# The first MLP product by pairs of feature chunks in seven block products instead of eight, with the residual kept in DRAM

## The chip, the cores and the metric

The kernel runs on one core of one Trainium2 chip. The metric is the device time of one execution in microseconds (us), as the median of three runs. A core has TensorE (PE in the profile, its weight loads apart as PEld), VectorE (DVE), ScalarE (ACT), GpSimd (POOL) and SyncE (SP, which here only issues transfers). Each runs its own list of instructions in a fixed order, and waits where an operand is not there yet.

## The reference

Two trunk layers run over 640 tokens (512 latent, 128 context) with 1024 features. What matters here is the second half of each layer, the MLP, and the modulation vectors that come from a product with `ada_w`:

```python
def ada_params(cond, w, b):
    m = jax.nn.silu(cond) @ w + b              # w: 1024 x 6144 for each layer
    return jnp.split(m[..., None, :], 6, axis=-1)
def mlp(h, w1, b1, w2, b2):                    # w1: 1024 x 4096, w2: 4096 x 1024
    return jnp.square(jax.nn.relu(h @ w1 + b1)) @ w2 + b2
for layer in range(2):
    ...                                        # mixer (even layer) or neighbourhood attention (odd)
    hp = modulate(xp, mp[3], mp[4])            # layer norm, times 1 + scale, plus shift
    hs = modulate(xs, ms[3], ms[4])
    xp = layer_norm(ALPHA * xp + mp[5] * mlp(hp, w1[layer], ...), ...)
    xs = layer_norm(ALPHA * xs + ms[5] * mlp(hs, w1[layer], ...), ...)
```

## The kernel before

All numbers are float32. Each operand of a product is split into a rounded part ("hi", type fp32r) and what the rounding left ("lo"), and a product is made of three matmuls: hi weights by hi data, hi by lo, lo by hi.

**Weights.** They come from DRAM in units of 128x1024 float32 (512 KB) in the order of a list (`stream_plan`). SP loads a unit into one of 3 `raw` slots; ACT copies it, rounded, into one of 4 `sp` slots (L170), and DVE subtracts the copy from the unit to get the lo half (L171). Up to two split units stand ready (`AHEAD`).

**The MLP** (`mlp`, L1026) of a layer runs over four blocks b of 1024 hidden features. Eight chunks m of 128 features of the first product come first: for a chunk, `ws` does 8 slices of 128 input features by 3 matmuls by 2 groups of tokens (384 and 256 columns), 48 matmuls in all; ACT adds the bias (L1020), DVE makes the squared ReLU (L1022), ACT and DVE split the result (`split_to`, L294 and L297). Then come 8 units of the second product (`tok_k_outer`, 30 matmuls of 512 columns for a unit). Its results are multiplied by a gate on DVE out of PSUM (L490) and added on POOL into the residual `x`, which lies in an SBUF slot R (L493): `evac_gated`. In the last block a `tail` does the second product together with the layer norm.

**The start of an MLP.** In block 0 the parts of chunks 0 to 3 for the first 384 tokens are computed first, while the last transposes and splits of the input `hT` (two R slots) still run. Then the gates are loaded, `make_base` scales the residual and adds the gated bias (POOL L504 twice, DVE L506 five times), and the 256-column rests of chunks 0 to 3 and the whole chunks 4 to 7 follow.

**The modulation of layer 1.** While layer 0's MLP runs, `ada_sum_gen` works through 48 steps, one for each weight unit: a 128x1024 piece of `ada_w` is loaded into an `n` slot, and DVE multiplies it by a factor and adds it to a sum, for two conditions (L428 for the first piece of a sum, then L430). Two loads stand ahead of the step at work. The R, `n` (6) and `vec` (4) slots of SBUF and the 8 banks of PSUM are given out by hand, a released slot going to the next user.

## Time and profile before

| | |
|---|---|
| median of three runs | 1514.3 us (1513.08 to 1514.66) |
| profiled execution, its own time | 1518.29 us |
| its span in the trace | 1516.2 us |
| PE busy | 1464.1 us, 97% of the span |
| DVE, ACT, POOL busy | 850.8, 594.4, 286.1 us |
| granted TensorE clock, mean | 0.984 |

The span is the time from the first to the last instruction in the trace; 2.1 us of the execution lie around it. Busy time is a sum over the whole program; what a stretch is worth has to be read from that stretch.

### The profile page before, as it was taken

Reading aid. Unit: us, or ns where it says so; the run is one execution under the profiler, and the core shown is the slowest. Engines: PE = TensorE matmul, PEld = TensorE weight load, DVE = VectorE, ACT = ScalarE, POOL = GpSimd, SP = SyncE. Lnnn points to the kernel's source line nnn. Section 1 sums busy time; section 2 is a strip of 40 time slices with the busy share of each in tenths; the row PEclk is TensorE's granted clock in tenths of the full one; section 3 lists DMA queues with packets and bytes.
Section 4 is the critical chain, followed back from the end, with each engine's and each line's share of the span. In section 5 each row is a group of like instructions: output and inputs, shape, how many; then the busy total and the mean of one; then the engine's idle time right before and its main releaser. Section 6 shows DMA issues by size and latency. Waiting matters only on the chain.

```text
span 1516.2 us, 21740 instructions
## 1 busy us (share of the span) xinstructions
PE 1464.1 (97%) x8572; PEld 1266.9 (84%) x8572; DVE 850.8 (56%) x1541; ACT 594.4 (39%) x1061; POOL 286.1 (19%) x327
## 2 busy tenths in 40 slices
...
GB/s 384 148 164 172 306 108 146 152 194 106 196 151 112 196 147 89 84 97 30 209 106 105 60 136 60 161 109 42 127 82 77 77 78 76 74 79 84 70 56 70
DMA packets 56373, 186.60 MB, mean 123 GB/s; under 512 B 10440, under 2 KB 10824, under 8 KB 56272
## 3 DMA queue, kind: packets, MB, share of 16 engines
...
q0 software_dynamic: 832, 1.09, 0.2%
...
## 4 chain that ended last, share of the span: by engine, by line
PE 76%; DVE 11%; ACT 5%; issue 4%; POOL 2%; DMA 2%; SPq 0%; POOLq 0%; DVEq 0%; ACTq 0%
PE bank L210 74%; DVE sp L171 2%; PE bank L1212 1%; POOL ln L514 1%; ACT R L755 1%; DVE R L506 1%; DVE R L297 1%; DVE R L495 1%; ACT junk L512 1%; DVE R L526 1%; DVE ln L533 1%; DVE acc L430 1%; ACT n L567 1%; DVE n L524 1%; POOL n L1202 1%
## 5 line engine op out<-in xcount | busy, mean ns | idle before, releaser
L210 PE MATMUL bank<-R,sp 128*128 128x384 f32 (+1 forms) x4368 | 664.5, 311 | 10.7 <-POOL R L296 3.6
L210 PEld LDWEIGHTS bank<-R,sp 128*128 128x128 f32 x4368 | 642.7, 190 | 28.4 <-issue 7.5
L210 PE MATMUL bank<-sp,R 128*128 128x512 f32 x2580 | 613.4, 396 | 7.1 <-DVE sp L171 2.6
L210 PEld LDWEIGHTS bank<-sp,R 128*128 128x128 f32 x2580 | 484.2, 189 | 128.3 <-issue 8.2
L171 DVE TENSOR_TENSOR sp<-raw,sp 128x1024 fp32r<-128x1024 f32 (+1 forms) x177 | 219.1, 1240 | 171.5 <-ACT sp L170 166.8
L170 ACT ACTIVATE sp<-raw 128x1024 fp32r<-128x1024 f32 (+1 forms) x177 | 186.1, 1056 | 316.0 <-PE bank L210 299.0
L493 POOL TENSOR_TENSOR R<-R,n 128x512 f32<-128x512 f32 x60 | 91.0, 1551 | 499.8 <-DVE n L490 499.8
L1022 DVE SCALAR_TENSOR_TENSOR n<-n 128x640 f32<-128x640 f32 x64 | 52.6, 822 | 189.3 <-ACT n L1020 189.3
L1020 ACT ACTIVATE n<-bank,pack 128x384 f32<-128x384 f32 (+1 forms) x128 | 61.2, 524 | 234.0 <-PE bank L210 228.4
L430 DVE SCALAR_TENSOR_TENSOR acc<-n,cx,acc 128x1024 f32<-128x1024 f32 x84 | 110.5, 1352 | 7.4 <-DMA n<-in_ada_w_dram 7.4
L297 DVE TENSOR_TENSOR R<-n,R 128x640 fp32r<-128x640 f32 (+2 forms) x123 | 98.6, 805 | 14.1 <-POOL R L296 11.1
L490 DVE TENSOR_TENSOR n<-bank,vec 128x512 f32<-128x512 f32 x100 | 67.3, 685 | 40.7 <-PE bank L210 36.6
L294 ACT ACTIVATE R<-n 128x640 fp32r<-128x640 f32 (+1 forms) x88 | 61.6, 704 | 44.3 <-DVE n L1022 39.5
L514 POOL TENSOR_TENSOR ln<-ln,mhalf 128x1 f32<-128x1 f32 x35 | 20.1, 575 | 296.8 <-DVE ln L513 296.8
L512 ACT ACTIVATE junk<-R,ln 128x1024 bf16<-128x1024 f32 x35 | 40.3, 1151 | 84.7 <-DVE ln L522 60.2
L210 PE MATMUL bank<-R,R 128*128 128x512 f32 x240 | 62.5, 405 | 0.0
L1202 POOL TENSOR_SCALAR n<-n,mx 128x384 f32<-128x384 f32 (+1 forms) x80 | 43.1, 541 | 91.1 <-DVE mx L1199 46.8
L567 ACT ACTIVATE n<-bank,mod 128x128 f32<-128x128 f32 x120 | 45.3, 455 | 26.5 <-PE bank L560 26.5
L210 PEld LDWEIGHTS bank<-R,R 128*128 128x128 f32 x240 | 44.4, 188 | 11.0
L1216 ACT ACTIVATE n<-bank 128x384 f32<-128x384 f32 (+1 forms) x80 | 32.9, 448 | 49.8 <-PE bank L1212 43.4
L1187 DVE CUSTOM_DVE_ANT_0 n<-bank,vec 128x256 f32<-128x256 f32 (+3 forms) x128 | 40.4, 350 | 13.2 <-PE bank L210 8.9
L1192 ACT ACTIVATE n<-n,mx 128x384 f32<-128x384 f32 x64 | 38.8, 610 | 20.4 <-DVE mx L1190 16.9
...
## 6 DMA issues: line engine op xcount, KB each, us to landing
raw<-in_wts_dram SPq DMA_DIRECT2D x184, 512.0 KB, 3.2
n<-in_ada_w_dram SPq DMA_DIRECT2D x80, 512.0 KB, 4.4
vec<-in_rpb_dram SPq DMA_DIRECT2D x16, 512.0 KB, 3.9
R<-in_ada_dram SPq DMA_DIRECT2D x15, 512.0 KB, 10.0
vec<-in_vecs_dram SPq DMA_DIRECT2D x13, 512.0 KB, 5.3
vec<-gscr SPq DMA_DIRECT2D x10, 512.0 KB, 4.8
R<-in_x_dram SPq DMA_DIRECT2D x5, 512.0 KB, 5.0
R<-in_xg_dram SPq DMA_DIRECT2D x5, 512.0 KB, 5.9
```

Of the source, the lines that this page charges most:

```text
L170: self.nc.scalar.activation(s.t[:, 0, :cols], r.t[:, :cols], AF.Copy)
L171: self.nc.vector.tensor_tensor(out=s.t[:, 1, :cols], in0=r.t[:, :cols], in1=s.t[:, 0, :cols].bitcast(F32), op=OP.subtract)
L210: self.nc.tensor.matmul(out, lhsT, rhs, start=start, stop=stop)
L294: self.nc.scalar.activation(hi, src, AF.Copy)
L297: (self.nc.vector if lo_eng == "dve" else self.nc.gpsimd).tensor_tensor(out=lo, in0=src, in1=hi.bitcast(F32), op=OP.subtract)
L430: nc.vector.scalar_tensor_tensor(acc.t[:, cond, :], w.t, f, acc.t[:, cond, :], op0=OP.mult, op1=OP.add)
L490: nc.vector.tensor_tensor(out=tmp.t[:, :512], in0=o.t, in1=gates[t // 4].t[:, c], op=OP.mult)
L493: nc.gpsimd.tensor_tensor(out=x[:, t, c], in0=x[:, t, c], in1=tmp.t[:, :512], op=OP.add)
L512: nc.scalar.activation(self.junk, src, AF.Square, bias=m[:, 2:3], accum_out=m[:, 4:5])
L567: nc.scalar.activation(dst, tr.t[:, j * 128:(j + 1) * 128], AF.Identity, bias=sh, scale=sc)
L1020: nc.scalar.activation(v[:, c0:c1], o.t[:, :c1 - c0], AF.Identity, bias=b)
L1202: nc.gpsimd.tensor_scalar(p.t[:, :n], p.t[:, :n], m[:, 5:6], 1.0, op0=OP.mult, op1=OP.mult)
```

## The change

The chunks m of 6 and above of each layer's first product (26 a layer, so 13 pairs a layer and 26 in all) are computed by pairs. For a pair the product is taken as 2x2 blocks: two chunks of 128 features, two halves of the 1024 input features, two halves of the 640 tokens. Seven block products of Winograd's form replace eight (`w1_pair`). A block product is 4 slices by 3 matmuls of 320 columns, so a pair has 84 matmuls where two chunks had 96. Around that:

- `split_pair`: a pair's two units become three and a half: POOL forms four 128x512 sums and differences in `vec` slots, and these are split too (ACT L172, DVE L173). Three may stand ready.
- `token_sums`, once a layer, in block 0 before `make_base`: POOL adds the hi and lo of `hT` (8 times 128x640), DVE forms 8 differences, and these are split (ACT, DVE) into two further R slots.
- The block products are combined on DVE out of PSUM, seven instructions of 320 columns; one of a pair's two results is split with its subtraction on POOL.
- The R slots for that come from the residual: after `make_base` it goes to DRAM (`xsum`, ten transfers of 256 KB), each gated result of the second product is added to it there by an accumulating DMA that POOL issues (`evac_sum`), and it is loaded back for the last block.
- The steps of `ada_sum_gen` run only within the second products of blocks 0 to 2 of layer 0, two for each unit. Of a step, one condition stays on DVE (L476, L479); for the other, ACT scales the piece and POOL adds it to the sum (128x1024, L481).

```diff
-ADA_MLP = 1
+ADA_MLP = 2
+PLAIN = 6
...
+    def paired(key):
+        return key[0] == "w1" and key[2] >= PLAIN
...
-        while len(self.ready) < self.AHEAD and (self.sp.free or self.extra) and self.raws:
-            r = self.raws.pop(0)
-            cols = 384 if self.plan[self.split_pos] == ("dft", 2) else 1024
+        while self.raws:
+            key = self.plan[self.split_pos] if self.split_pos < len(self.plan) else None
+            pair = self.paired(key)
+            if len(self.ready) >= (3 if pair else self.AHEAD) or not (self.sp.free or self.extra):
+                break
+            if pair and self.sub == 0 and len(self.raws) < 2:
+                break
             s = self.sp.get([128, 2, 1024], F32R) if self.sp.free else self.extra.pop(0)
-            with self.tc.high_priority(SPLIT_PRI):
-                self.nc.scalar.activation(s.t[:, 0, :cols], r.t[:, :cols], AF.Copy)
-                self.nc.vector.tensor_tensor(out=s.t[:, 1, :cols], in0=r.t[:, :cols],
-                                             in1=s.t[:, 0, :cols].bitcast(F32), op=OP.subtract)
-            r.done()
+            if pair:
+                self.split_pair(s)
+            else:
+                r = self.raws.pop(0)
+                cols = 384 if key == ("dft", 2) else 1024
+                self.split_unit(s, r.t, cols)
+                r.done()
+                self.split_pos += 1
...
+    def split_pair(self, s):
+        nc = self.nc
+        r = self.raws
+        if self.sub == 0:
+            r0, r1 = r[0].t, r[1].t
+            self.sums = [self.vec.get([128, 1024]) for _ in range(2)]
+            s1, s2 = (self.sums[0].t[:, i * 512:(i + 1) * 512] for i in range(2))
+            s3, s4 = (self.sums[1].t[:, i * 512:(i + 1) * 512] for i in range(2))
+            self.split_unit(s, r0, 1024)
+            nc.gpsimd.tensor_tensor(out=s1, in0=r1[:, :512], in1=r1[:, 512:], op=OP.add)
+            nc.gpsimd.tensor_tensor(out=s2, in0=s1, in1=r0[:, :512], op=OP.subtract)
+            nc.gpsimd.tensor_tensor(out=s3, in0=r0[:, :512], in1=r1[:, :512], op=OP.subtract)
+            nc.gpsimd.tensor_tensor(out=s4, in0=r0[:, 512:], in1=s2, op=OP.subtract)
+            r.pop(0).done()
+        elif self.sub < 3:
+            self.split_unit(s, self.sums[self.sub - 1].t, 1024)
+            self.sums[self.sub - 1].done()
+        else:
+            self.split_unit(s, r[0].t[:, 512:], 512)
+            r.pop(0).done()
+            self.split_pos += 2
+        self.sub = (self.sub + 1) % 4
...
-        if self.ada_every and self.seen % self.ada_every == 0:
+        for _ in range(self.ada_every):
             next(self.ada, None)
...
+            f = [self.s[:, k, cond:cond + 1] for cond in range(2)]
+            if k == 0:
+                nc.vector.tensor_scalar(acc.t[:, 0, :], w.t, f[0], None, op0=OP.mult)
+                nc.scalar.activation(acc.t[:, 1, :], w.t, AF.Copy, scale=f[1])
+            else:
+                nc.vector.scalar_tensor_tensor(acc.t[:, 0, :], w.t, f[0], acc.t[:, 0, :], op0=OP.mult, op1=OP.add)
+                nc.scalar.activation(w.t, w.t, AF.Copy, scale=f[1])
+                nc.gpsimd.tensor_tensor(out=acc.t[:, 1, :], in0=acc.t[:, 1, :], in1=w.t, op=OP.add)
...
+    def block_mm(self, s, off, B, c0):
+        o = self.psum()
+        v = o.t[:, :self.HT]
+        for c in range(4):
+            w = slice(off + c * 128, off + (c + 1) * 128)
+            hi, lo = B.t[:, c, 0, c0:c0 + self.HT], B.t[:, c, 1, c0:c0 + self.HT]
+            self.mm(v, s.t[:, 0, w], hi, c == 0, False)
+            self.mm(v, s.t[:, 0, w], lo, False, False)
+            self.mm(v, s.t[:, 1, w], hi, False, c == 3)
+        return o, v
+    def token_sums(self, hT):
+        nc = self.nc
+        H2 = self.HT
+        T12, T34 = (self.R.get([128, 4, 2, T], F32R) for _ in range(2))
+        def full(i, j, g):
+            f = self.n.get([128, 1024])
+            v = f.t[:, :2 * H2].rearrange("p (c q) -> p c q", c=2)
+            hi, lo = (hT[i].t[:, 2 * g:2 * g + 2, w, j * H2:(j + 1) * H2].bitcast(F32) for w in range(2))
+            nc.gpsimd.tensor_tensor(out=v, in0=hi, in1=lo, op=OP.add)
+            return f, v
+        def put(dst, j, g, v):
+            hi, lo = (dst.t[:, 2 * g:2 * g + 2, w, j * H2:(j + 1) * H2] for w in range(2))
+            self.split_to(hi, lo, v)
+        for g in range(2):
+            fa, a = full(0, 1, g)
+            fb, t1 = full(0, 0, g)
+            nc.vector.tensor_tensor(out=t1, in0=a, in1=t1, op=OP.subtract)
+            put(T12, 0, g, t1)
+            fc, t2 = full(1, 1, g)
+            nc.vector.tensor_tensor(out=a, in0=t2, in1=a, op=OP.subtract)
+            put(T34, 0, g, a)
+            fa.done()
+            nc.vector.tensor_tensor(out=t2, in0=t2, in1=t1, op=OP.subtract)
+            put(T12, 1, g, t2)
+            fb.done()
+            fd, t4 = full(1, 0, g)
+            nc.vector.tensor_tensor(out=t4, in0=t2, in1=t4, op=OP.subtract)
+            put(T34, 1, g, t4)
+            fc.done()
+            fd.done()
+        return T12, T34
+    def w1_pair(self, l, m, hT, sums, dst):
+        nc = self.nc
+        H2 = self.HT
+        T12, T34 = sums
+        b = [self.pack[:, PC_B1 + l * 32 + m + i:PC_B1 + l * 32 + m + i + 1] for i in range(2)]
+        f = [self.n.get([128, 1024]) for _ in range(2)]
+        c11, c12, t1 = (f[0].t[:, i * H2:(i + 1) * H2] for i in range(3))
+        c21, c22, u2 = (f[1].t[:, i * H2:(i + 1) * H2] for i in range(3))
+        assert self.plan[self.pos][0] == "w1" and self.plan[self.pos][1:] == (l, m), self.plan[self.pos]
+        self.pos += 2
+        stt, tt = nc.vector.scalar_tensor_tensor, nc.vector.tensor_tensor
+        def out(i):
+            v = f[i].t[:, :T]
+            nc.vector.scalar_tensor_tensor(v, v, 0.0, v, op0=OP.max, op1=OP.mult)
+            self.split_to(dst[i][:, 0, :], dst[i][:, 1, :], v, lo_eng=("dve", "pool")[i])
+            f[i].done()
+        s = self.next_sub()
+        o, p = self.block_mm(s, 0, hT[0], 0)
+        nc.scalar.activation(t1, p, AF.Copy)
+        o.done()
+        o, p = self.block_mm(s, 512, hT[1], 0)
+        stt(c11, p, b[0], t1, op0=OP.add, op1=OP.add)
+        o.done()
+        s.done()
+        s = self.next_sub()
+        o, p = self.block_mm(s, 512, T12, H2)
+        tt(out=u2, in0=p, in1=t1, op=OP.add)
+        o.done()
+        o5, p5 = self.block_mm(s, 0, T12, 0)
+        tt(out=c12, in0=p5, in1=u2, op=OP.add)
+        s.done()
+        s = self.next_sub()
+        o, p = self.block_mm(s, 0, T34, 0)
+        stt(c21, p, b[1], u2, op0=OP.add, op1=OP.add)
+        o.done()
+        tt(out=c22, in0=p5, in1=c21, op=OP.add)
+        o5.done()
+        o, p = self.block_mm(s, 512, hT[1], H2)
+        stt(c12, p, b[0], c12, op0=OP.add, op1=OP.add)
+        o.done()
+        s.done()
+        s = self.next_sub()
+        out(0)
+        o, p = self.block_mm(s, 0, T34, H2)
+        tt(out=c21, in0=c21, in1=p, op=OP.subtract)
+        o.done()
+        s.done()
+        self.pump()
+        out(1)
+    def evac_sum(self, o, t, n, gates):
+        nc = self.nc
+        tmp = self.n.get([128, 1024])
+        nc.vector.tensor_tensor(out=tmp.t[:, :512], in0=o.t, in1=gates[t // 4].t[:, n * 512:(n + 1) * 512], op=OP.mult)
+        o.done()
+        nc.gpsimd.dma_start(out=self.xsum[t][n], in_=tmp.t[:, :512], accum_op=OP.add)
+        tmp.done()
...
+                sums = self.token_sums(hT)
                 self.make_base(x.t, gates, b2)
                 b2.done()
-            for m in range(8):
+                for t in range(NT):
+                    for n in range(2):
+                        nc.sync.dma_start(out=self.xsum[t][n], in_=x.t[:, t, n * 512:(n + 1) * 512])
+                x.done()
+                if l == 0:
+                    self.ada = self.ada_sum_gen(1)
+                    next(self.ada)
+            h1.append(self.R.get([128, 4, 2, T], F32R))
+            hs = self.chunks(h1)
...
+                self.ada_every = ADA_MLP if l == 0 else 0
                 for n in range(2):
                     outs = self.tok_k_outer([("w2", l, b, n, k) for k in range(4)], range(4), hs)
                     for t in range(NT):
-                        self.evac_gated(outs[t], x.t, t, n, gates)
+                        self.evac_sum(outs[t], t, n, gates)
+                self.ada_every = 0
             else:
-                for r in hT:
+                for r in [*hT, *sums]:
                     r.done()
+                x = self.R.get([128, NT, D])
+                for t in range(NT):
+                    for n in range(2):
+                        nc.sync.dma_start(out=x.t[:, t, n * 512:(n + 1) * 512], in_=self.xsum[t][n])
```

**How instructions stand on DVE at the start of layer 1's MLP.** The rows below are from the kernel before, from the last split of the input `hT` (R1, R4) to the split of chunk 4's unit, `sp3_120`, which PE needs after the rests of chunks 0 to 3.

```order
L297 TENSOR_TENSOR R1_37_9145<-n2_344_9619,R1_37_9145 128x4x128
L297 TENSOR_TENSOR R4_38_9146<-n2_344_9619,R4_38_9146 128x4x128
L506 SCALAR_TENSOR_TENSOR R2_35_8832<-R2_35_8832,n5_345_9698 128x1024
L506 SCALAR_TENSOR_TENSOR R2_35_8832<-R2_35_8832,n1_346_9704 128x1024
L1022 SCALAR_TENSOR_TENSOR n3_347_9732<-n3_347_9732 128x640
L171 TENSOR_TENSOR sp3_120_9831<-raw2_126_9464,sp3_120_9831 128x1024
```

After the change the split of chunk 4's unit is `sp1_146`. The first row below is the last split into the first half of `hT` (R1); R4 and R2 are the two slots of token sums, R0 is the residual, R3 the first hidden slot. They are 31 rows in all; those left out are of the same lines.

```order
L346 TENSOR_TENSOR R1_40_9351<-n0_352_9824,R1_40_9351 128x4x128
L1110 TENSOR_TENSOR n5_354_9907<-n1_353_9905,n5_354_9907 128x640
L346 TENSOR_TENSOR R5_41_9352<-n0_352_9824,R5_41_9352 128x4x128
L346 TENSOR_TENSOR R4_43_9903<-n5_354_9907,R4_43_9903 128x2x320
L1113 TENSOR_TENSOR n1_353_9905<-n2_355_9912,n1_353_9905 128x640
L346 TENSOR_TENSOR R2_44_9904<-n1_353_9905,R2_44_9904 128x2x320
...
L1120 TENSOR_TENSOR n5_360_9940<-n1_359_9932,n5_360_9940 128x640
L556 SCALAR_TENSOR_TENSOR R0_38_9038<-R0_38_9038,n4_362_9951 128x1024
L1072 SCALAR_TENSOR_TENSOR n3_363_9990<-n3_363_9990 128x640
L346 TENSOR_TENSOR R3_42_9740<-n3_363_9990,R3_42_9740 128x640
L1072 SCALAR_TENSOR_TENSOR n5_366_10083<-n5_366_10083 128x640
L173 TENSOR_TENSOR sp1_146_10089<-raw2_126_9670,sp1_146_10089 128x1024
```

Between the last split into the first half of `hT` and chunk 4's split stood 1 split, 2 rows of `make_base` and 1 squared ReLU; now there stand 8 differences and their 8 splits, 1 split of `hT`, 5 rows of `make_base`, 4 squared ReLUs and 3 splits of results. Layer 0 has the same list before `sp3_28`, its chunk 4.

**DVE and POOL at the end of a second product in layer 0.** The rows below are from DVE before, at the end of block 1's second product: results are gated (L490), a sum of `ada_w` ends (L455), and the next begins with two steps.

```order
L490 TENSOR_TENSOR n4_162_4110<-bank5_167_3970,vec3_10_2429 128x512
L490 TENSOR_TENSOR n5_163_4113<-bank7_168_3977,vec2_11_2431 128x512
L455 TENSOR_TENSOR n3_164_4118<-bank2_169_4121,n3_164_4118 128x512
L428 TENSOR_SCALAR acc0_5_4127<-n0_157_4025,cx_1_108 128x1024 x2
L430 SCALAR_TENSOR_TENSOR acc0_5_4127<-n1_158_4064,cx_1_108,acc0_5_4127 128x1024 x2
L171 TENSOR_TENSOR sp2_59_4206<-raw0_61_4030,sp2_59_4206 128x1024
L430 SCALAR_TENSOR_TENSOR acc0_5_4127<-n0_165_4130,cx_1_108,acc0_5_4127 128x1024 x2
```

After the change, on DVE, at the end of block 1's second product and into the first pair of block 2 (`sp3_68` and `sp0_69` hold its third and fourth split):

```order
L479 SCALAR_TENSOR_TENSOR acc0_4_4037<-n1_162_4099,cx_1_118,acc0_4_4037 128x1024
L173 TENSOR_TENSOR sp3_68_4200<-vec0_24_4108,sp3_68_4200 128x1024
L479 SCALAR_TENSOR_TENSOR acc0_4_4037<-n3_163_4150,cx_1_118,acc0_4_4037 128x1024
L1183 TENSOR_TENSOR n5_167_4233<-bank6_179_4056,vec3_10_2417 128x512
L1183 TENSOR_TENSOR n0_168_4236<-bank4_180_4063,vec3_10_2417 128x512
L1183 TENSOR_TENSOR n2_169_4239<-bank0_181_4070,vec3_10_2417 128x512
L1183 TENSOR_TENSOR n4_170_4242<-bank2_182_4077,vec3_10_2417 128x512
L173 TENSOR_TENSOR sp0_69_4252<-raw1_59_4054,sp0_69_4252 128x512
L479 SCALAR_TENSOR_TENSOR acc0_4_4037<-n1_164_4155,cx_1_118,acc0_4_4037 128x1024
L1183 TENSOR_TENSOR n5_171_4245<-bank3_183_4084,vec2_11_2419 128x512
L1150 SCALAR_TENSOR_TENSOR n0_172_4250<-bank5_185_4271,pack_75,n0_172_4250 128x320
```

And on POOL at the same place, where before there were only the adds into the residual (L493) and one issue of a transfer:

```order
L481 TENSOR_TENSOR acc0_3_3819<-acc0_3_3819,n3_149_3926 128x1024
L1185 DMA xsum1_0_67<-n4_154_4016 128x512
L1185 DMA xsum2_0_69<-n5_155_4019 128x512
L481 TENSOR_TENSOR acc0_3_3819<-acc0_3_3819,n1_150_3931 128x1024
L1185 DMA xsum3_0_71<-n0_156_4022 128x512
L1185 DMA xsum4_0_73<-n2_157_4025 128x512
L207 TENSOR_TENSOR vec1_23_4107<-raw1_59_4054 128x512
L209 TENSOR_TENSOR vec0_24_4108<-raw0_58_3981,raw1_59_4054 128x512
L208 TENSOR_TENSOR vec1_23_4107<-vec1_23_4107,raw0_58_3981 128x512
L210 TENSOR_TENSOR vec0_24_4108<-raw0_58_3981,vec1_23_4107 128x512
L513 DMA gscr_63<-n4_158_4028 16x1x32 x4
L481 TENSOR_TENSOR acc0_4_4037<-acc0_4_4037,n1_152_3976 128x1024
```

The splits of the pair now stand among steps of the `ada_w` sum, each of which waits for its piece, and the slot of a piece comes free only after ACT's scaling and POOL's add (L481). The issues of the accumulating DMAs (L1185) stand behind those adds on POOL, and the fifth gated result (`n5_171`) takes the slot of the first (`n5_167`), which that DMA has to have read.

## Rows read from the trace of the kernel before

**Rows 1.** Page: busy time by engine; share of the chain that ended last.

```profile
PE 1464.1 (97%) x8572; PEld 1266.9 (84%) x8572; DVE 850.8 (56%) x1541; ACT 594.4 (39%) x1061; POOL 286.1 (19%) x327
...
PE 76%; DVE 11%; ACT 5%; issue 4%; POOL 2%; DMA 2%; SPq 0%; POOLq 0%; DVEq 0%; ACTq 0%
```

**Rows 2.** Timeline of PE, layer 1, one block: start, length, line, count.

```profile
1177.45 55.27 PE L210 MATMUL bank<-R,sp 128*128 128x384 f32 x384
1232.57 54.86 PE L210 MATMUL bank<-sp,R 128*128 128x512 f32 x240
1287.26 2.98 PE L210 MATMUL bank<-R,sp 128*128 128x384 f32 x19
```

**Rows 3.** Timeline of DVE and PE, start of layer 1's MLP.

```profile
1077.83 1.09 DVE L297 TENSOR_TENSOR R<-n,R 128x512 fp32r<-128x512 f32 x1
1078.85 1.21 DVE L506 SCALAR_TENSOR_TENSOR R<-R,n 128x1024 f32<-128x1024 f32 x1
1079.99 1.70 DVE L297 TENSOR_TENSOR R<-n,R 128x512 fp32r<-128x512 f32 x2
1088.33 1.23 DVE L171 TENSOR_TENSOR sp<-raw,sp 128x1024 fp32r<-128x1024 f32 x1
...
1077.65 45.28 PE L210 MATMUL bank<-R,sp 128*128 128x384 f32 x323
1122.77 2.44 PE L210 MATMUL bank<-sp,R 128*128 128x512 f32 x10
```

**Rows 4.** Single lines: shortest, median and longest ns, first and last start.

```profile
L493 POOL TENSOR_TENSOR R<-R,n x60: 1281/1302/2357, 342.9 to 1398.7; 128x512 f32<-128x512 f32 x60
L504 POOL TENSOR_TENSOR n<-vec,vec x8: 2353/2399/3356, 176.5 to 1072.9; 128x1024 f32<-128x1024 f32 x8
L766 POOL TENSOR_TENSOR R<-R,R x8: 1557/1567/4678, 72.3 to 125.3; 128x640 f32<-128x640 f32 x8
L430 DVE SCALAR_TENSOR_TENSOR acc<-n,cx,acc x84: 1266/1277/3393, 259.8 to 575.3; 128x1024 f32<-128x1024 f32 x84
L171 DVE TENSOR_TENSOR sp<-raw,sp x177: 1193/1224/2566, 14.5 to 1467.9; 128x1024 fp32r<-128x1024 f32 x176, 128x384 fp32r<-128x384 f32 x1
L1022 DVE SCALAR_TENSOR_TENSOR n<-n x64: 807/825/827, 281.5 to 1453.4; 128x640 f32<-128x640 f32 x64
```

**Rows 5.** Timelines of POOL and of DVE, layer 0, 342 to 350 us.

```profile
342.88 8.12 POOL L493 TENSOR_TENSOR R<-R,n 128x512 f32<-128x512 f32 x4 [69.43 <-DVE n L490]
...
343.32 1.95 DVE L430 SCALAR_TENSOR_TENSOR acc<-n,cx,acc 128x1024 f32<-128x1024 f32 x1
345.19 0.68 DVE L490 TENSOR_TENSOR n<-bank,vec 128x512 f32<-128x512 f32 x1
345.79 1.73 DVE L430 SCALAR_TENSOR_TENSOR acc<-n,cx,acc 128x1024 f32<-128x1024 f32 x1
348.64 1.21 DVE L171 TENSOR_TENSOR sp<-raw,sp 128x1024 fp32r<-128x1024 f32 x1
```

**Rows 6.** Timeline of DVE and PE, start of layer 0's MLP.

```profile
272.90 1.09 DVE L297 TENSOR_TENSOR R<-n,R 128x512 fp32r<-128x512 f32 x1
287.52 1.21 DVE L171 TENSOR_TENSOR sp<-raw,sp 128x1024 fp32r<-128x1024 f32 x1
...
288.79 27.56 PE L210 MATMUL bank<-R,sp 128*128 128x384 f32 x186 [1.43 <-DVE sp L171]
```

**Rows 7.** Windows: length, busy PE, PEld, DVE, ACT, POOL, granted clock, DMA.

```profile
257.00:316.00 59.00, 54.92 (x372) 54.19 (x372) 51.64 (x51) 26.67 (x47) 12.97 (x8) 0.97 0.55 183
431.00:487.00 56.00, 56.00 (x249) 45.12 (x248) 36.70 (x36) 9.95 (x11) 15.36 (x12) 1.00 0.46 151
1060.00:1122.00 62.00, 59.46 (x394) 58.77 (x393) 40.41 (x46) 30.66 (x54) 11.43 (x10) 0.94 0.34 115
```

**Rows 8.** Groups of instructions by shape; page: DMA issues with time to landing.

```profile
L170 ACT ACTIVATE sp<-raw 128x1024 fp32r<-128x1024 f32 x176 | 185.7, 1059 | 316.0 <-PE bank L210 299.0 <-DMA raw<-in_wts_dram 16.9
L1187 DVE CUSTOM_DVE_ANT_0 n<-bank,vec 128x320 f32<-128x320 f32 x32 | 15.4, 481 | 1.5 <-PE bank L210 1.5
...
n<-in_ada_w_dram SPq DMA_DIRECT2D x80, 512.0 KB, 4.4
...
out_new_v_dram<-R POOLq DMA_DIRECT2D x2, 256.0 KB, 6.8
```

49 lines of the change are left out of this document (28 added, 21 removed).

## The prediction, made before the changed kernel was run

> **What bounds the kernel now.** I read the page first: PE is busy for 97% of the span, and 76% of the chain that ended last is PE [rows 1]. The timeline of PE shows how tight that is: a block of eight chunks is one run of 384 matmuls from 1177.45 to 1232.57 us, and the second product follows at once, 240 matmuls to 1287.26 [rows 2]. In these blocks whatever PE no longer has to do comes off the time, as long as the splits, sums and results keep up. So the question is where DVE and POOL are late after the change, and for that I read the starts of the two MLPs, where the change puts new work in front of PE [rows 3, 6], and layer 0's second products, where it puts the `ada_w` sums [rows 7].
>
> **What the change removes: 44.8 us of PE.** A block's 384 matmuls take 55.12 us, 143.5 ns each at a mean of 320 columns [rows 2]. The new matmuls all have 320 columns, so I give each the same. Two chunks cost 96 x 143.5 = 13.78 us, a pair 84 x 143.5 = 12.05 us; 1.72 us less for each of 26 pairs makes 44.8 us.
>
> **How POOL and DVE get in each other's way.** This sets most prices below, so it comes first. Four adds of POOL that alone take 1.30 us each (median) [rows 4] needed 8.12 us where DVE ran steps of the `ada_w` sum between them; those took 1.95 and 1.73 us instead of 1.28 [rows 4, 5]. Alone, the four adds (5.2 us) and the three DVE instructions with two SBUF operands (1.28, 1.28, 1.22) are 9.0 us of work, and it took 8.1 us: one after the other, with some 0.3 us of overlap for each pair of them. The gating in the same stretch, which reads PSUM and one SBUF operand, kept its 0.68 us. So I count instructions of DVE with two SBUF operands and POOL adds as one queue, less 0.3 us for each change of hands. The Trainium skill, SBUF — State Buffer, section "Who interferes with whom", says the same as a rule: a VectorE instruction with two SBUF inputs and a GpSimd instruction that reads SBUF exclude each other for their whole length, and one with a single SBUF input does not contend. By that rule, too, the new POOL adds are not free cover, and the trace's 8.12 us agrees; without it the change would be a gain (the second rival).
>
> **The start of each MLP: +47 us, and 4 for the clock.** In layer 1 PE began its long run at 1077.65 and had done all eight chunks at 1122.77 [rows 3]; chunks 4 to 7 are 4 x 6.89 = 27.6 us of that, so PE wants chunk 4's split at 1095.2. It stood ready early, begun at 1088.33. After the change DVE has 30 instructions from the last split into the first half of `hT`, which ended at 1077.83 + 1.09 = 1078.9, to the end of chunk 4's split: 8 differences, 11 splits and 4 squared ReLUs of 640 elements at 0.825 us (19.0; the median of L1022, which has this size) [rows 4], one split of `hT` (0.85, half of 1.70) [rows 3], five of `make_base` at 1.21 us (6.1) [rows 3], and the split itself, 1.22. That is 27.1 us. Nearly all have two SBUF operands. Against them stand on POOL six additions of 640 elements that come after the last part of `hT`, at 1.57 us, and two products of `make_base` at 2.40: 14.2 us [rows 4]. As one queue that makes 41.3, less 8 x 0.3 = 39.0 us; chunk 4's split ends at 1117.9 and PE waits 22.7 us. Layer 0 has the same list: from 272.90 + 1.09 = 274.0 to 313.0, where the split ended at 288.73 and PE already lost 1.43 us behind it [rows 6], so 24.3 us more. The bounds: with no exclusion at all 27.1 us, giving 10.8 and 12.4; with no overlap 25.0 and 26.6. Nothing covers this on PE, whose order has only the 256-column rests ahead. The wait idles PE, and after the idle stretches at these places the granted clock was 0.94 over 62 us and 0.97 over 59 [rows 7]; 3% to 6% of some 60 us is 2 to 4 us, of which a part is paid already, so 2 us each.
>
> **Layer 0's second products: +27 us.** Blocks 0 to 2 each get 16 steps of the `ada_w` sum in 8 units, where there were 8 at two DVE instructions each. In such a block DVE was busy for 36.7 us and POOL for 15.4 of 56 [rows 7]. After: POOL has 14 adds of 1024 at 2.40 and 8 of 512 at 1.30 for the two first pairs (44.0 us), DVE 14 steps at 1.28 and 8 splits at 1.22 (27.7). As one queue 71.7, less 22 x 0.3, 65 us for a block that PE does in 54.7. The chain of one step asks for more: load of the piece 4.4 us, step 1.28, ACT's scaling about 1.06 (as L170), add 2.40: 9.1 us [rows 4, 8], and with two slots 4.6 us a step, 73 us for 16. The next pair's third and fourth split stand behind these steps, so PE cannot run far past them; it has about a pair's blocks of room. Of the 10 to 18 us I take 13 for blocks 1 and 2 each. Of block 0's steps the order puts six ahead among the pairs, so 10 x 4.6 = 46 us fit: 1 us. Below, the bound is 0 (the steps hide as they did); above, 18 for all three with the pairs behind them held up too.
>
> **Pairs elsewhere: +3 us.** One pair gives DVE 3.5 splits (4.3), two squared ReLUs and one split of a result (2.5) with two SBUF operands, and seven combinations out of PSUM at 0.48 (the nearest of 320 elements) [rows 8]: 10.2 us in 12.05. With POOL's four sums and one split (6.8) the queue is 13.6, less 5 x 0.3, 12.1 us: level with PE. I take half a microsecond for each of the six w1 blocks made only of pairs; bounds 0 and 6 each.
>
> **The residual through DRAM: 0.** The 60 adds leave POOL, 60 issues come. No accumulating DMA is in the trace; the nearest is a 256 KB transfer issued by POOL that landed after 6.8 us [rows 8]. A result's slot has to wait for that, but the next user of it comes five results later, a token tile apart, and PE has 8 banks; in layer 1 nothing else uses these slots. The reload of `x` stands at the head of the last block's second product, whose first result is needed only after two units. Between 0 and 2 us; I take 0.
>
> **Sum.** -44.8 + 22.7 + 24.3 + 4 + 27 + 3 = +36 us. The profiled execution took 1518.3 us with a span of 1516.2; that makes 1554 for a profiled one, and on the median of 1514.3, 1550 us.
>
> **Rivals.**
> - *The queue is worse than I count (layer 0 paced by the steps).* If the two slots pace all three second products and each pair block is paced by 13.6 us a pair, 5 us more come in blocks 1 and 2 each, 17 in block 0, and 6 in each of the three pair blocks: 45 us on top, 1595 us. For it speaks that each step passes through four engines in turn; against it that DVE and POOL can catch up within a pair block of layer 0, which no longer holds steps.
> - *POOL and DVE work side by side (faster).* Then the starts cost 10.8 + 12.4 = 23.2 us, the products little (44 us on POOL and 27.7 plus ten gatings of 0.68 on DVE, in 54.7), about 1 elsewhere: -44.8 + 24.2 = -20.6, 1494 us. It decides the sign once the starts and the products together cost less than 44.8 us. Against it stand the 8.12 us for four adds [rows 5].
> - *Everything hides*: 1514.3 - 44.8 = 1469.5 us. Then chunk 4's split would have to come before the token sums, and the order on DVE says it doesn't.
> - *Between*: the starts as I say (47), the products nearly hidden: 1500 to 1530 us. For it speaks that a block's slack on DVE was 19 us.
>
> **Chances.** My forecast (1530 to 1570) 0.50; the worse queue (1570 to 1600) 0.15; between (1500 to 1530) 0.16, of which 0.04 lie within 0.2%, 0.05 below and 0.07 above; side by side 0.15; everything hides 0.04. Faster by over 0.2% (3 us, about what a measurement can tell): 0.15 + 0.04 + 0.05 = 0.24; the same 0.04; slower 0.72. The range runs from 1492 to 1592: it leaves out the last case, half of the side-by-side case and a sixth of the worse queue, under 0.2. The forecast's own range is 1530 to 1570.
>
> **What would show it.** Right: the 143.5 ns hold for matmuls of 320 columns; PE stands idle for 20 to 25 us ahead of the first matmul of chunk 4 in both layers, released by DVE's split; POOL's additions of 640 elements and DVE's differences never run at once; in layer 0's second products of blocks 1 and 2, PE waits on the third or fourth split of a pair while POOL is busy almost throughout. Wrong: PE without a gap there, POOL adds at 1.30 and 2.40 us beside DVE splits, or an idle PE in layer 1's later blocks, which would mean that the accumulating DMAs or the combinations out of PSUM are the late ones.

## The result and the profile after

The changed kernel takes 1619.4 us (median of four runs, 1618.13 to 1620.58) against 1513.73 (median of four too): a ratio of 1.070, interval 1.068 to 1.072. The profiled execution has a span of 1618.8 us against 1516.2, so 102.6 us to account for. I forecast the sign and 36 us; the range ended at 1592.

The page of the changed kernel, with busy time and the chain that ended last:

```profile
PE 1456.4 (90%) x8260; PEld 1241.4 (77%) x8260; DVE 1036.6 (64%) x1733; ACT 660.5 (41%) x1099; POOL 586.2 (36%) x515
...
PE 43%; DVE 16%; issue 8%; DMA 8%; POOL 5%; ACT 4%; SPq 0%; POOLq 0%; DVEq 0%; ACTq 0%
```

PE's share of the chain fell from 76% to 43% [rows 1]; VectorE, transfers, GpSimd and issue have 37% where they had 19%. PE is busy for only 8 us less though it has fewer matmuls: it ran part of them at a lower granted clock.

The places where the time went are seen when each stretch of PE's timeline, from the first matmul of one kind to the first of the next, is set against the kernel before (us):

| stretch | before | after | difference |
|---|---|---|---|
| up to the last part of chunk 3 of layer 0 | 268.5 | 264.0 | -4.5 |
| layer 0, first block's first product | 48.7 | 68.2 | +19.5 |
| second product b0, pairs b1, second product b1 | 170.8 | 207.8 | +37.0 |
| pairs b2, second product b2, pairs b3 | 171.3 | 212.3 | +41.0 |
| tail, layer 1's attention | 418.3 | 417.2 | -1.1 |
| layer 1, first block's first product | 45.1 | 67.6 | +22.5 |
| three second products, three pair blocks | 329.6 | 316.4 | -13.2 |
| last second product to the end | 63.8 | 65.2 | +1.4 |

**Layer 1 behind its start** is the change as meant. PE's timeline there, to set beside [rows 2]:

```profile
1292.06 37.45 PE L259 MATMUL bank<-R,sp 128*128 128x320 f32 x254
1330.74 12.28 PE L259 MATMUL bank<-R,sp 128*128 128x320 f32 x82 [1.23 <-DVE sp L173]
1342.86 55.11 PE L259 MATMUL bank<-sp,R 128*128 128x512 f32 x240
```

A pair block takes 50.8 us where eight chunks took 55.1. A matmul of 320 columns takes 37.45/254 = 147.4 ns, not 143.5, so a pair saves 1.4 us and not 1.72.

**The start of layer 1's MLP.** Timelines of DVE, ACT, POOL and PE, to set beside [rows 3]:

```profile
1191.73 3.37 DVE L556 SCALAR_TENSOR_TENSOR R<-R,n 128x1024 f32<-128x1024 f32 x1
...
1208.39 1.21 DVE L173 TENSOR_TENSOR sp<-raw,sp 128x1024 fp32r<-128x1024 f32 x1
...
1191.84 0.74 ACT L343 ACTIVATE R<-n 128x640 fp32r<-128x640 f32 x1 [4.78 <-DVE n L1113]
...
1195.87 0.95 ACT L1070 ACTIVATE n<-bank,pack 128x384 f32<-128x384 f32 x2 [2.34 <-DVE R L346]
...
1171.86 1.57 POOL L1100 TENSOR_TENSOR n<-R 128x640 f32<-128x640 f32 x1 [0.88 <-DVE R L346]
...
1191.15 2.86 POOL L554 TENSOR_TENSOR n<-vec,vec 128x1024 f32<-128x1024 f32 x1 [0.76 <-DVE R L346]
...
1196.50 2.90 PE L259 MATMUL bank<-R,sp 128*128 128x384 f32 x8 [8.64 <-ACT n L1070]
1200.47 1.44 PE L259 MATMUL bank<-R,sp 128*128 128x320 f32 x4 [1.07 <-ACT n L1070]
1209.65 27.61 PE L259 MATMUL bank<-R,sp 128*128 128x384 f32 x168 [7.75 <-DVE sp L173]
```

From 1171.86, where the first half of the input is split and POOL's sums begin, to the end of chunk 4's split at 1209.60 is 37.7 us; I had 39.0. PE waits in two pieces: first 9.7 us for ACT (L1070), which stands behind a split of a token sum (L343, a wait of 4.78 us) and then waits 2.34 us for a slot that the sums give back, and then 7.75 us for chunk 4's split. The 3.37 us of a 1.21 us instruction (L556) are POOL's 2.86 us product beside it.

**Layer 0.** Windows of the changed kernel (length, busy PE, PEld, DVE, ACT, POOL, granted clock, DMA share, GB/s); the first product of block 0, its second product, pairs and second product of block 1 and of block 2, and a pair block of layer 1:

```profile
247.70:332.20 84.50, 62.49 (x388) 59.88 (x389) 67.45 (x69) 40.67 (x68) 38.47 (x25) 0.84 0.35 117
332.20:404.30 72.10, 59.25 (x254) 47.00 (x253) 46.11 (x42) 23.73 (x23) 42.40 (x22) 0.91 0.58 166
404.30:466.00 61.70, 54.59 (x346) 52.09 (x344) 47.42 (x54) 19.49 (x26) 31.06 (x20) 0.94 0.40 105
466.00:540.00 74.00, 63.86 (x256) 48.44 (x253) 41.70 (x39) 22.46 (x22) 37.32 (x23) 0.91 0.57 164
540.00:615.10 75.10, 56.45 (x346) 53.42 (x344) 52.05 (x59) 24.20 (x31) 41.76 (x25) 0.89 0.38 106
615.10:698.70 83.60, 64.34 (x261) 49.53 (x257) 50.26 (x47) 26.13 (x25) 45.44 (x24) 0.88 0.55 157
...
1292.10:1342.90 50.80, 49.57 (x338) 49.23 (x337) 41.93 (x48) 20.06 (x26) 21.22 (x14) 1.00 0.38 98
```

In layer 0, where PE waits between matmuls, the granted clock is 0.84 to 0.94 in these windows. Before, it was 0.97 at the first product and 1.00 in block 1's second product [rows 7], and 1.00 in block 2's, in the same window view:

```profile
546.20:602.80 56.60, 56.60 (x257) 45.57 (x253) 37.65 (x41) 9.92 (x10) 14.19 (x9) 1.00 0.42 135
```

Block 2's second product now keeps PE busy for 64.3 us at 0.88; the same matmuls took 56.6 us before. The other 19 us of that stretch are waits. What VectorE and GpSimd lost shows in the groups by shape:

```profile
L173 DVE TENSOR_TENSOR sp<-raw,sp 128x1024 fp32r<-128x1024 f32 x150 | 213.5, 1427 | 121.3 <-ACT sp L172 120.7
L481 POOL TENSOR_TENSOR acc<-acc,n 128x1024 f32<-128x1024 f32 x42 | 112.8, 2686 | 62.0 <-ACT n L480 61.7
L479 DVE SCALAR_TENSOR_TENSOR acc<-n,cx,acc 128x1024 f32<-128x1024 f32 x42 | 81.7, 1945 | 70.9 <-DMA n<-in_ada_w_dram 70.8
```

A step on DVE takes 1.95 us on average, where the median before was 1.28 [rows 4]. And these are the waits of PE itself, in timelines of SP, DVE and PE in block 2's second product:

```profile
662.20 0.54 SPq L496 DMA_DIRECT2D n<-in_ada_b_dram  x1
...
671.42 1.28 DVE L479 SCALAR_TENSOR_TENSOR acc<-n,cx,acc 128x1024 f32<-128x1024 f32 x1 [9.31 <-DMA n<-in_ada_w_dram]
...
674.05 0.69 DVE L505 TENSOR_TENSOR n<-bank,n 128x512 f32<-128x512 f32 x1 [1.35 <-DMA n<-in_ada_b_dram]
...
656.02 1.92 PE L259 MATMUL bank<-acc,ones 128*32 128x512 f32 x4 [6.69 <-DVE acc L479]
...
674.80 1.12 PE L518 MATMUL bank<-ident,n 128*128 128x128 f32 x4 [7.84 <-DVE n L505]
```

PE's own list holds the ends of the `ada_w` sums, matmuls with ones and transposes, in the middle of a second product. PE waits there once for the eighth step of the sum, once for a bias (`ada_b`) that is loaded only when the sum ends. Ahead of that bias DVE had waited 9.31 us for a piece of `ada_w` that SP asked for only after `ada_b` had its slot, and then 1.35 us for `ada_b` itself: a late slot in SP's list holds up both.

### The profile page after: what moved, and what is told of

Its sections match the earlier page's. It is cut to its first block, busy times and chain, and to the rows that moved or that the text cites. A ratio compares the mean times of both kernels' runs of the same rounds, so it can differ in the third digit from the quotient of the medians.

```text
span 1618.8 us, 21981 instructions
## 1 busy us (share of the span) xinstructions
PE 1456.4 (90%) x8260; PEld 1241.4 (77%) x8260; DVE 1036.6 (64%) x1733; ACT 660.5 (41%) x1099; POOL 586.2 (36%) x515
## 4 chain that ended last, share of the span: by engine, by line
PE 43%; DVE 16%; issue 8%; DMA 8%; POOL 5%; ACT 4%; SPq 0%; POOLq 0%; DVEq 0%; ACTq 0%
PE bank L259 41%; DVE sp L173 4%; DMA n<-in_ada_w_dram 3%; DVE R L346 2%; POOL acc L481 2%; DMA xsum<-n 2%; DVE n L1141 1%; PE bank L1392 1%; DVE R L556 1%; ACT sp L172 1%; DMA raw<-in_wts_dram 1%; POOL ln L564 1%; DVE acc L479 1%; DMA n<-in_ada_b_dram 1%; POOL n L1100 1%
## 5 line engine op out<-in xcount | busy, mean ns | idle before, releaser
L259 PE MATMUL bank<-R,sp 128*128 128x320 f32 (+3 forms) x4056 | 640.0, 317 | 78.0 <-ACT n L1070 24.0
L259 PEld LDWEIGHTS bank<-sp,R 128*128 128x128 f32 x2580 | 488.7, 192 | 139.3 <-issue 13.2
L173 DVE TENSOR_TENSOR sp<-raw,sp 128x1024 fp32r<-128x1024 f32 (+2 forms) x177 | 243.8, 1381 | 121.3 <-ACT sp L172 120.7
L172 ACT ACTIVATE sp<-raw 128x1024 fp32r<-128x1024 f32 (+2 forms) x177 | 173.2, 987 | 166.1 <-PE bank L259 126.0
L343 ACT ACTIVATE R<-n 128x640 fp32r<-128x640 f32 (+1 forms) x104 | 73.2, 709 | 217.6 <-DVE n L1141 165.9
L481 POOL TENSOR_TENSOR acc<-acc,n 128x1024 f32<-128x1024 f32 x42 | 112.8, 2686 | 62.0 <-ACT n L480 61.7
L479 DVE SCALAR_TENSOR_TENSOR acc<-n,cx,acc 128x1024 f32<-128x1024 f32 x42 | 81.7, 1945 | 70.9 <-DMA n<-in_ada_w_dram 70.8
L346 DVE TENSOR_TENSOR R<-n,R 128x640 fp32r<-128x640 f32 (+2 forms) x113 | 104.2, 932 | 22.6 <-POOL R L345 19.3
L480 ACT ACTIVATE n<-n,cx 128x1024 f32<-128x1024 f32 x42 | 48.3, 1150 | 146.5 <-DVE acc L479 146.3
L173 DVE TENSOR_TENSOR sp<-vec,sp 128x1024 fp32r<-128x1024 f32 x52 | 74.1, 1426 | 51.2 <-ACT sp L172 48.8
L346 POOL TENSOR_TENSOR R<-n,R 128x640 fp32r<-128x640 f32 x26 | 41.4, 1591 | 155.2 <-ACT R L343 149.5
L207 POOL TENSOR_TENSOR vec<-raw 128x512 f32<-128x512 f32 x26 | 39.2, 1506 | 160.4 <-DMA raw<-in_wts_dram 98.7
L172 ACT ACTIVATE sp<-vec 128x1024 fp32r<-128x1024 f32 x52 | 53.6, 1051 | 75.7 <-PE bank L259 55.0
L1185 POOL DMA_DIRECT2D xsum<-n x60 | 56.5, 1199 | 55.0 <-DVE n L1183 54.8
L562 ACT ACTIVATE junk<-R,ln 128x1024 bf16<-128x1024 f32 x35 | 40.2, 1149 | 87.4 <-DVE ln L572 59.6
```

Source lines behind the costliest of these rows:

```text
L172: self.nc.scalar.activation(s.t[:, 0, :cols], src[:, :cols], AF.Copy)
L173: self.nc.vector.tensor_tensor(out=s.t[:, 1, :cols], in0=src[:, :cols], in1=s.t[:, 0, :cols].bitcast(F32), op=OP.subtract)
L259: self.nc.tensor.matmul(out, lhsT, rhs, start=start, stop=stop)
L343: self.nc.scalar.activation(hi, src, AF.Copy)
L346: (self.nc.vector if lo_eng == "dve" else self.nc.gpsimd).tensor_tensor(out=lo, in0=src, in1=hi.bitcast(F32), op=OP.subtract)
L479: nc.vector.scalar_tensor_tensor(acc.t[:, 0, :], w.t, f[0], acc.t[:, 0, :], op0=OP.mult, op1=OP.add)
```

## The experiments

Three theories. **A**: the pace of the `ada_w` steps, by GpSimd's adds against VectorE (A1, exclusion) or by the way of a piece through two slots (A2, ring). **C**: the accumulating DMAs hold slots, so that the `ada_b` load and PE behind it are late. And the token sums stand ahead of chunk 4. (The first expectations call A2 "theory A" and A1 "theory B"; from no_ada on, theory A is the pace of the steps from either.) Lengths of layer 0's stretches in each run but late_sums and l1_pairs, which are told below (second products b0, b1, b2 and pair blocks b1, b2, b3, in order of time), and their sum:

| run | time | b0 | b1 pairs | b1 | b2 pairs | b2 | b3 pairs | sum |
|---|---|---|---|---|---|---|---|---|
| before (chunks for pairs) | 1513.7 | 56.6 | 58.1 | 56.1 | 58.1 | 56.6 | 56.6 | 342 |
| changed | 1619.4 | 72.1 | 61.6 | 74.1 | 75.0 | 83.6 | 53.6 | 420 |
| own_dve | 1576.2 | 69.1 | 52.1 | 62.7 | 67.5 | 76.7 | 51.1 | 379 |
| three_slots | 1620.5 | 73.9 | 58.8 | 68.7 | 74.2 | 85.0 | 52.5 | 413 |
| before_ada (no pairs) | 1556.7 | 63.6 | 57.6 | 73.4 | 57.6 | 73.8 | 58.6 | 385 |
| pool_memset | 1576.5 | 69.6 | 50.3 | 65.4 | 58.7 | 78.2 | 55.1 | 377 |
| no_add | 1577.8 | 69.6 | 54.1 | 59.6 | 67.5 | 79.4 | 51.1 | 381 |
| no_ada | 1560.4 | 69.4 | 52.0 | 63.5 | 51.3 | 75.7 | 51.1 | 363 |
| no_ada_ab | 1539.7 | 61.4 | 50.7 | 61.8 | 54.0 | 60.1 | 51.1 | 339 |
| ab_early | 1611.9 | 65.1 | 73.9 | 69.2 | 71.5 | 74.3 | 58.4 | 412 |
| own_ab | 1582.3 | 61.4 | 61.7 | 61.7 | 71.0 | 65.3 | 61.8 | 383 |
| own_ab_halves | 1573.3 | 56.6 | 65.9 | 61.8 | 70.9 | 61.3 | 59.1 | 376 |
| spread | 1583.5 | 64.1 | 67.1 | 56.1 | 77.2 | 66.1 | 53.3 | 384 |
| both8 | 1530.9 | 62.7 | 61.4 | 56.8 | 67.6 | 57.2 | 66.1 | 372 |

**The ada part alone (before_ada)**: the kernel before, with the changed step and its new place (two steps for each unit, in the second products alone); the step is shown.

```diff
-                    nc.vector.scalar_tensor_tensor(acc.t[:, cond, :], w.t, f, acc.t[:, cond, :], op0=OP.mult,
-                                                   op1=OP.add)
+                nc.vector.scalar_tensor_tensor(acc.t[:, 0, :], w.t, f[0], acc.t[:, 0, :], op0=OP.mult, op1=OP.add)
+                nc.scalar.activation(w.t, w.t, AF.Copy, scale=f[1])
+                nc.gpsimd.tensor_tensor(out=acc.t[:, 1, :], in0=acc.t[:, 1, :], in1=w.t, op=OP.add)
```

> The kernel before with the ada_w part of the change alone: two steps per unit in layer 0's second products only, ScalarE's scaling and GpSimd's add for one condition; no pairs, no token sums, residual in SBUF. Theories A and B: the second products of blocks 0 to 2 take about 70 us instead of 55 and the starts stay as they were: 1514 + 45 = 1560. Theory C (accumulating DMAs): they are not here, so within 10 us of the kernel before.

It costs 41 us without pairs and without accumulating DMAs (ratio 1.027, 1.024 to 1.030). Blocks 1 and 2 take 73.4 and 73.8 us, the 73 us that the prediction worked out for the ring and then took as 68. PE's timeline in its block 1 shows where:

```profile
435.89 26.12 PE L210 MATMUL bank<-sp,R 128*128 128x512 f32 x113
471.76 1.92 PE L210 MATMUL bank<-acc,ones 128*32 128x512 f32 x4 [9.75 <-DVE acc L430]
476.02 1.92 PE L210 MATMUL bank<-acc,ones 128*32 128x512 f32 x4 [2.34 <-POOL acc L432]
```

**Ring or exclusion (own_dve, three_slots, pool_memset, no_add).** own_dve puts the second condition back on VectorE, in place of the last two + lines above, in the changed kernel. The others, each alone:

```diff
-            while i < len(todo) and len(q) < 2:
+            while i < len(todo) and len(q) < 3:
...
-                nc.gpsimd.tensor_tensor(out=acc.t[:, 1, :], in0=acc.t[:, 1, :], in1=w.t, op=OP.add)
+                nc.gpsimd.memset(w.t, 0.0)
+                nc.gpsimd.memset(w.t, 0.0)
...
-                nc.gpsimd.tensor_tensor(out=acc.t[:, 1, :], in0=acc.t[:, 1, :], in1=w.t, op=OP.add)
```

> The changed kernel, but both conditions of an ada_w step are summed on VectorE again (ScalarE's scaling and GpSimd's add undone; still two steps per unit of layer 0's second products). Theory A, the ring of two slots: a piece's slot comes back only after load, VectorE step, scaling and add, so a step takes half of that ring; without scaling and add the ring is 4.4 + 2.55 = 7 us, 3.5 us a step, 56 us for 16. Layer 0's second products fall from 72, 74 and 84 us to 56 to 60, the pair blocks behind them to about 52: some 75 us less, 1545. Theory B, GpSimd's adds shut VectorE out: the adds are gone too, VectorE then has 41 us of steps, 10 of splits and 7 of gating in 55, so 58 to 60 us a block: about the same, 1550. Theory C, the accumulating DMAs hold slots and the SP queue: nothing changes much, over 1600.

> The changed kernel with three pieces of ada_w loaded ahead instead of two; engines and adds as in the change. Theory A (ring): 9.1 us through three slots is 3.0 us a step, 49 us for 16, so the second products of layer 0 come to 55 to 60 us and some 60 us come back: 1555. Theory B (GpSimd's adds and VectorE's instructions in one queue): that queue stays 65 us long in a block that PE does in 55, so only 10 to 25 us come back: 1595 to 1610. Theory C (DMAs hold slots): one slot fewer for the rest makes it worse, over 1620.

> The changed kernel with each of the 42 adds on GpSimd (L481) replaced by two writes of zeros over the scaled piece: a piece still passes through load, VectorE, ScalarE and GpSimd before its slot is free, but GpSimd reads nothing there. The sum for that condition is left out, so layer 1's modulation is not the reference's. Exclusion (GpSimd's adds that read SBUF and VectorE's two-operand instructions shut each other out): VectorE's step falls from 1.95 us on average to about 1.35, its splits from 1.38 to 1.27, and 25 to 45 us come back: 1575 to 1595, near the run with VectorE's own steps. Ring or GpSimd's time (the piece's way through four engines): little changes, 1610 or more.

> The changed kernel without the 42 adds on GpSimd (the sum for one condition is left out, so layer 1's modulation is not the reference's): load, VectorE's step and ScalarE's scaling stay, with half of VectorE's work of the run with its own steps. The pace of the steps is then 4.4 + 1.3 + 1.1 = 6.8 us by two slots, 3.4 us. If the late ada_b load is the limit that is left: near the run without steps, 1560 to 1570. If the steps still set the pace: 1590 or more.

A third slot gave back nothing (1620.5). By itself that doesn't rule out the ring, since the slot comes out of the same six that hold the results. DVE's waits from 330 to 720 us (total, times, longest), in the changed kernel and with three slots:

```profile
DVE acc L479 <- DMA n<-in_ada_w_dram: 70.6, 28, 9.3
DVE n L1183 <- DMA xsum<-n: 7.9, 3, 4.2
```

```profile
DVE n L1183 <- DMA xsum<-n: 36.1, 10, 8.3
DVE acc L479 <- DMA n<-in_ada_w_dram: 10.3, 9, 2.8
```

The waits for pieces went, and waits for a result's slot came. own_dve gave 43 us, less than either theory expected. With writes instead of adds, a piece still passes all four engines and GpSimd is busy for 2.04 us per step, and again 43 us came back (ratio to the kernel before 1.041, 1.036 to 1.046). pool_memset, groups by shape (the second write, L482, takes as long as the first):

```profile
L479 DVE SCALAR_TENSOR_TENSOR acc<-n,cx,acc 128x1024 f32<-128x1024 f32 x42 | 62.6, 1490 | 42.9 <-DMA n<-in_ada_w_dram 42.7
L481 POOL MEMSET n<- 128x1024 f32 x42 | 42.9, 1021 | 78.4 <-ACT n L480 78.2
```

The step fell from 1.95 to 1.49 us, and two writes are 0.65 us shorter than an add. So a piece's way is some 1.1 us shorter, which through two slots and 42 steps is an estimated 23 us at most: the ring could be a part of the 43. Against that stands no_add, where the way is 2 us shorter again and no more came back (1577.8). This speaks for A1: what costs is that the add reads SBUF beside VectorE. That the adds cost 43 us is shown; that no part of it is the ring's is argued. The Trainium skill, SBUF — State Buffer, section "Who interferes with whom", says that a GpSimd instruction which only writes SBUF doesn't contend with a two-operand VectorE instruction; the 43 us agree.

**The late ada_b (no_ada, ab_early, no_ada_ab).** no_ada leaves out 42 of the 48 steps; ab_early asks for the slot and the loads at the fourth step; no_ada_ab is both.

```diff
+            if k > 0:
+                if k == 7:
+                    fin = self.ada_sum_finish(l, p, acc)
+                yield
+                continue
...
+            if k == 3:
+                ab = self.n.get([128, 1024])
+                b = self.a["ada_b"]
+                for cond in range(2):
+                    nc.sync.dma_start(out=ab.t[cond * 64:(cond + 1) * 64, :512], in_=bass.AP(
+                        tensor=b.tensor, offset=b.offset + l * 6144 + p * 1024, ap=[[512, 2], [0, 32], [1, 512]]))
```

> The changed kernel without 42 of the 48 ada_w steps: only the first piece of each of the six sums is loaded and multiplied, so layer 1's modulation vectors are not the reference's; the ends of the sums (matmuls with ones, transposes) stay. Theory A (the pace of the steps): layer 0's second products fall to 55 us and its pair blocks to 51, 99 us less: 1520. Theory C (accumulating DMAs hold the slots that the ends of the sums and the pairs need): waits of 10 us for the ends of the sums stay, 1545 or more.

> The changed kernel with the slot and the two small loads of ada_b asked for at the fourth step of a sum instead of after its eighth. PE's four waits for transposes behind that load were 27.6 us. Theory C (the load waits for a slot that an accumulating DMA holds, and PE for the load): these waits go, and with them some of the lower clock: 30 to 38 us less, 1585. Theory A (the steps' pace bounds the blocks anyway): PE waits as long somewhere else, 1605 to 1620.

> The run without 42 of the 48 ada_w steps (so layer 1's modulation is not the reference's), and with the slot and loads of ada_b asked for at the fourth step's place. Without the steps alone the second products of layer 0 still took 69, 64 and 76 us, and PE waited 29.5 us for the ends of the sums. Theory C (the ada_b load waits for a slot held by an accumulating DMA, PE for the load): these go, second products 55 to 58 us, 1520 to 1525. Rival (PE waits for something else at these places, such as the result slots themselves): 1545 to 1560.

Without steps the second products still took 69, 64 and 76 us: theory A alone is not enough, and theory C's forecast (1545 or more) held. PE's waits from 200 to 720 us in no_ada and, from 330 to 720, in no_ada_ab (total, times, longest):

```profile
PE bank L526 <- DVE n L513: 29.5, 4, 10.6
```

```profile
PE bank L533 <- DVE n L520: 8.8, 4, 3.3
```

The chain behind it, in own_dve's timelines of DVE, SP and PE:

```profile
623.49 0.69 DVE L1182 TENSOR_TENSOR n<-bank,vec 128x512 f32<-128x512 f32 x1 [3.64 <-DMA xsum<-n]
...
624.81 1.10 SPq L495 DMA_DIRECT2D n<-in_ada_b_dram  x2
...
635.96 0.69 DVE L504 TENSOR_TENSOR n<-bank,n 128x512 f32<-128x512 f32 x1 [6.88 <-DMA n<-in_ada_b_dram]
...
636.71 1.11 PE L517 MATMUL bank<-ident,n 128*128 128x128 f32 x4 [11.05 <-DVE n L504]
```

The fifth result waits for the first one's DMA to land, `ada_b` gets its slot after that, its load needs 10 us, and PE stands for 11. The accumulating DMAs hold only part of these slots. SP's waits for `ada_b`'s slot in the changed kernel, 330 to 720 us:

```profile
SPq L496 <- DMA xsum<-n: 20.9, 3, 8.5
SPq L496 <- DVE n L1173: 6.2, 1, 6.2
SPq L496 <- DVE R L346: 5.8, 1, 5.8
```

Two of the others are for results of a pair (L1173, L346). Asked for early, the stretches without steps fall from 363 to 339 us (1560 to 1540). With all steps in place the same edit gives only 8, as theory A forecast: the two causes hide each other. What is left in no_ada_ab, 339 us where 342 less 12 pairs at 1.39 would be 325, is not taken apart.

**Both mended (own_ab, own_ab_halves).** own_dve with early `ada_b`; then also two results to a slot:

```diff
-        tmp = self.n.get([128, 1024])
+        if t % 2 == 0:
+            self.tmp = self.n.get([128, 1024])
+        v = self.tmp.t[:, t % 2 * 512:t % 2 * 512 + 512]
```

> Both conditions of a step on VectorE (GpSimd's adds gone) and ada_b asked for early. By the two causes together (pace of the steps with GpSimd, late ada_b) both are mended: second products 56 to 60 us, pair blocks 51 to 53: 1535. If VectorE with 41 us of steps, 10 of splits and 7 of gating is itself too long, 60 to 65 us a second product: 1550 to 1560. Neither alone did more than 43 us.

> As the run with VectorE's steps and early ada_b, and two gated results share one slot, so that five results need three slots and none waits for an accumulating DMA to land. If those landings (VectorE waited 25 us for them in the run with early ada_b alone) hold up VectorE: 10 to 20 us less than that run. If they are covered: within 5 us of it.

Misses: 1582 us, no better than own_dve and above both forecasts, and 1573 with shared slots, 9 less, just under the 10 to 20 of its first forecast. The second products do fall to 61 to 65 us, but the pair blocks rise to 62, 71 and 62. What the steps push back now falls there: in block 2's pairs PE waits 7.0 us at one go for a gating on DVE (L1183) and 13.5 us in all, at a granted clock of 0.90. VectorE has little room there (42 of 50.8 us in layer 1's pair blocks, without steps), but it isn't full: it was busy for 49 to 58 of these 62 to 71 us. It waited 26.9 us for accumulating DMAs to free a result's slot (330 to 720 us), and with shared slots not at all.

**The ada part undone (spread)**: own_dve, one step per unit over the whole MLP, two per pair.

```diff
+        for _ in range(2 * self.ada_every):
+            next(self.ada, None)
```

> The changed kernel with the ada_w part undone wholly: both conditions on VectorE, one step per unit over layer 0's MLP, two per pair. Theory A: the second products go back to 56 to 57 us; a pair block has two steps of 2.55 us per pair beside VectorE's 10.2, 15.3 us for a pair that PE does in 12.05, so 61 us for the blocks 1 and 2: 1540 to 1545. Theory C: the ends of the sums still wait for a slot that an accumulating DMA has to release: 1560 or more.

1583.5 us: theory A's forecast is missed by 40, theory C's (1560 or more) held. Pair blocks of 67 and 77 us were expected at 61, and PE waited 37.1 us for the ends of the sums.

**The token sums (late_sums)**, written after chunk 5:

```diff
-                sums = self.token_sums(hT)
                 self.make_base(x.t, gates, b2)
...
+                if sums is None and m == PLAIN:
+                    sums = self.token_sums(hT)
                 if self.paired(("w1", l, b * 8 + m)):
```

> The changed kernel with the token sums written after chunk 5 instead of ahead of make_base, so that the splits of chunks 4 and 5 need not wait for them. If the 19.5 and 22.5 us that the first blocks gained come from chunk 4's split standing behind the sums, PE runs through chunk 5 without a gap: 35 to 40 us less, 1580. The rival: the sums (39 us of VectorE and GpSimd in turn) only move, and the first pair waits for them, since PE reaches it 14 us after chunk 4: then 15 to 20 us less, 1600.

The rival was right, and too mild: 7.5 us. Layer 1's first stretch, counted from its first matmul, shrinks from 85.0 to 74.3 us, but in layer 0 PE waits 20.2 us for the sums at the first pair instead.

**Pairs where there is room (l1_pairs, both8).** Pairs from each second block on, token sums after the first block's first product; l1_pairs in layer 1 alone, with layer 0 as before; both8 in both, with VectorE's steps, early `ada_b`, shared slots and steps spread by hand.

```diff
-        return key[0] == "w1" and key[2] >= PLAIN
+        return key[0] == "w1" and key[1] == 1 and key[2] >= PLAIN
...
+            if sums is None and l == 1:
+                sums = self.token_sums(hT)
             if b < NFB - 1:
```

> Pairs in layer 1 alone, from its second block on (12 pairs), token sums after the first block's first product, residual in DRAM for layer 1; layer 0 as in the kernel before. If what the change loses comes from the sums ahead of chunk 4 and from the ada_w steps, nothing is left to lose: three blocks of 50.5 us instead of 55.1 and a tail 1.4 us longer, 1502. If the token sums cost in whatever place, or the first second product of layer 1 waits for them, 1514 or more.

> Pairs in both layers from the second block on (24 pairs), token sums after the first block's product, both conditions on VectorE, ada_b early, results two to a slot, and the 48 steps spread by hand: one per unit in block 0, 13 in each second product of blocks 1 and 2, six beside pairs. If the causes named are all, both layers get the 13 us that layer 1 alone got: 1490. If VectorE is full in layer 0 (50 of 55 us in the second products): 1500 to 1515, no better than pairs in layer 1 alone.

l1_pairs takes 1501.4 us, ratio 0.991 (0.988 to 0.994), as expected (1502): the one version below both kernels, by 0.9% of the kernel before. Its timeline of PE, from the first second product of layer 1:

```profile
1119.26 54.84 PE L259 MATMUL bank<-sp,R 128*128 128x512 f32 x240
1173.94 37.53 PE L259 MATMUL bank<-R,sp 128*128 128x320 f32 x254
1212.69 12.29 PE L259 MATMUL bank<-R,sp 128*128 128x320 f32 x82 [1.22 <-DVE sp L173]
```

PE doesn't wait at all for token sums there. both8 is 1530.9 (1.010, 1.007 to 1.012), above both forecasts. In it no stretch of layer 0 from the first second product to the last pairs beats the kernel before; that this is because the steps share VectorE with them is argued.

## Why the prediction was wrong

- **The gain of 44.8 us**: mis-sized. 147.4 ns a matmul gives 26 x 1.39 = 36.2.
- **The start of each MLP, +47 and 4 for the clock, less a pair each**: right. I had 47.6 us for both stretches net of the pairs; 42.0 were measured (19.5 and 22.5). In layer 1 the split came 37.7 us after the input, for 39.0, and chunk 4 began 22.6 us later than before, for 22.7 (in layer 0 20.7, for 24.3). I had named DVE's split as the only releaser; 9.7 of the 17.5 us that PE stood in layer 1, and 14.3 of 20.2 in layer 0, were for ACT (L1070).
- **"Layer 0's second products: +27 us" is the step that failed**, with "the residual through DRAM: 0" behind it. For the six stretches I had 7.8 us (27 + 1.5 less 12 pairs' 20.7); they lost 78. First, the steps alone cost 41 us (before_ada): I had worked out 73 us a block and took 68, and 1 us for block 0 where 7 came. I reasoned that PE could run on past the steps by a pair's blocks. It can't: PE's own list holds the end of each sum. Second, I priced the accumulating DMAs by their landing, 6.5 us measured for my 6.8, and asked who uses the result's slot next only among the results. For three of the six sums the next user was `ada_b`, and PE waits for that. Third, the clock: I charged 2 us at each start, and none in these stretches, where it fell to 0.88 to 0.94. In the five stretches at these clocks PE was busy for 298 us, where the same work took some 270 at 1.00. Nor did the sign come that PE would wait for a pair's third or fourth split while POOL is busy almost throughout: from 330 to 720 us PE waited 40 us for the ends of the sums and 19 for splits, and in block 2's second product POOL was busy for 45 of 83.6 us.
- **The mechanism of exclusion** was right: without the adds that read SBUF, 43 us come back. The ring, which I used for the size, gave 73 us a block, and 73.4 and 73.8 were measured without pairs (before_ada); since no run shows the ring as the limit, that agreement may be luck.
- **The first rival (1595)** had the right place and side, and the steps at their full 73 us a block. Its price left out the late `ada_b` and the clock.
- **Layer 1's pair blocks, +0.5 each**: 1.2 us or less of waiting each; right.
